# A two-layer hybrid encoder: state space matmuls in line behind the sixth gate, weight splits ranked ahead, outputs grouped by shape, parameters loaded with the projections

## The chip, the cores and the metric

One core of a Trainium2 chip. A core has a matmul engine (TensorE, in rows PE, with PEld for its weight loads), a vector engine (VectorE, DVE), an activation engine (ScalarE, ACT), GpSimd (POOL), and queues that issue DMAs (SyncE, SP, above all). Each engine works through its own list of instructions in order. The metric is the device time of one execution, in microseconds (us).

## The reference, cut to what matters

Two equal layers over a (1, 1024, 1024) float32 input. Each layer takes a root-mean-square norm, one projection to 2504 columns, three token mixers, a SiLU gate on each mixer's output, and one output projection with a residual:

```python
h = rms_norm(x, norm_g[l]); proj = h @ w_in[l]
ya = dsa_branch(...)     # 6 heads, an indexer picks the 256 best keys of each query
yb = s5_branch(u, ...)   # state space: 16 groups of 16 channels, 64 complex states each
yc = mla_branch(...)     # 6 heads, low-rank queries and keys
mixed = concat([ya * silu(ga), yb * silu(gb), yc * silu(gc)])
x = x + mixed @ w_out[l]
```

The state space branch computes, with `abar = exp(a * step)` complex and diagonal, `x_t = abar x_(t-1) + f (B u_t)` and `y_t = Re(C x_t) + D u_t`, then a GELU and a gated linear unit.

## The kernel before, in words

Every matmul of the large projections is split: the float32 weights become a rounded part `whi` and a remainder `wlo`, the activations `hh` and `hl`, and three products are added (`proj_step`, `mm3`). A weight tile arrives by DMA as `raw`; `split_act` (L152) makes `whi` on ACT (L153) and `wlo` on POOL, for some on DVE (L154). `class Stream` (L597) loads the tiles of a layer some four or five ahead and splits them three ahead.

A layer runs so. `norm_tile` and `turn_h` make the transposed `hh` (ACT, L686) and `hl` (DVE, L687) in two halves of four token tiles, `jk` being the normed tile (DVE, L664). `proj_halves` is the first projection, on each half of the tokens in turn. After two projections come the steps of the string `STEPS = "L5C6Q7U01234"` (L49): a letter is a projection, a digit is a gate of 128 channels, and U is the input of the state space branch, two such channels. A gate or U channel has two halves of 24 matmuls of 512 columns (`gt`, L166 to L168). A gate's half is read by ACT (`th`, a tanh, L1182) and by DVE (`gate`, L1183), after which its PSUM bank is free. The tag `s` of PSUM has six banks, shared by projections, gates and later the attention scores; the tag `tr` has two. The sixth gate in this order is "2"; gates "3" and "4" follow it, and then 48 attention items (24 for the indexed heads, then 24 for the latent heads, `scores` and `finish`), and the output projection (`po`).

Beside that run generators, called sides. A side is advanced by `tick` (L574): every projection step, gate matmul group or attention item adds its planned microseconds to a clock, and a side whose due time has come traces its next piece; what it yields is the time until the piece after. One side is the indexer with its search for the 256 best keys (`index_topk`), mostly DVE. Another is the state space branch (`tables_then_s5`, L1189), begun before U; its yields are stretched by `S5M = 1.5`. For each of two halves of the groups, `static` (L401) makes tables (`s5t` on POOL, `s5o`, called `Wf`, on DVE, both at L279), yields `ST3`, and then goes on with matmuls of a 48-column kernel table (L425), the band matrix `M` by DMAs (L437), transposes (L442) and rotation tables on POOL (L264 to L269). `chunks` (L462) makes two PSUM tiles from U (L471), multiplies them by the rotation on DVE (L479 to L486), scans them (L489, L490) and turns them back on POOL to the states `X`; it ends with a yield of `ST2`. `outputs` (L498) adds in PSUM, for each four groups of 16 channels, `U M` (128 rows, L508) and two products of `X` with `Wf` (64 rows, L509, L510), each of which is two passes of the engine, and applies the GELU (ACT L513, L516; DVE L514, L515, L517). When both halves are through, the gated linear unit follows (L547 to L560) and the product with the gate (L1195).

`s5_params` (L285), once in layer 0 for both layers, loads three small tensors by SP (L292) and computes the powers of `abar` in some 125 tiny DVE instructions (tiles `zp`, `s5par`), two memsets on POOL, and stores the result by one DMA (L356). Before the change its loads are traced among the loads of the input, between input tiles 3 and 4, and the rest is a side with due time 1.0. Only the first exponential is held (`issue_after(late[0])`) behind the last `hl` traced until then.

The order on each engine comes from the planner of the framework: it simulates the program on a timeline of its own and lets each engine take, among the instructions whose inputs are there by that timeline, the one of the best rank. The rank is the order of tracing (`tc.cur_priority`, which can be shifted by hand). Where the chip is slower than that timeline, an engine stands before an instruction whose input is late, and all behind it stand too.

Of the kernel before, what the change touches and what calls it, by code (L numbers as in the profile page):

```python
# [24 lines left out]
AHEAD = 3  # L25
DEEP = 2
S5AT = 2
KVAT = 22
KVT = 1.5
EVA = 0.9  # L30
# [19 lines left out]
S5W = (0, 0)  # L50
S5M = 1.5
FT = 0.6
ST2 = 8.0
ST3 = 4.0
GLP = 0
KTP = (0, 0, 0)
# [30 lines left out]
def hybrid_kernel(ctx, tc, A, out, dbg=None, layers=DEPTH):  # L87
# [17 lines left out]
    def ps_s(shape, name="s"):  # L105
        return pp.tile(shape, F32, tag="s", name=name, bufs=BANKS)
# [45 lines left out]
    def split_act(raw, hi, lo, eng=None):  # L152
        S.activation(hi, raw, AF.Copy)  # L153
        (eng or G).tensor_tensor(lo, raw, f(hi), op=ALU.subtract)  # L154
# [130 lines left out]
    def s5_params():  # L285

        zp.clear()
        o = page([128, 1024], F32, "s5par")[:, 0:560].rearrange("p (l c) -> p l c", l=2)

        def load(n):  # L290
            t = tiny("s5" + n)
            nc.sync.dma_start(t, A["ssm_" + n].rearrange("l p g -> p l g"))  # L292
            return t
        ar, ai, ls = (load(n) for n in ("a_re", "a_im", "log_step"))
        yield 0.1
        with tc.issue_after(late[0]):
            step = exp_acc(ls, "ze")
        e1, th = tiny("e1"), tiny("th")
        V.tensor_tensor(e1, ar, step, op=ALU.mult)
        V.tensor_tensor(th, ai, step, op=ALU.mult)  # L300
        yield 2.0
        mag = exp_acc(e1, "zm")
        yield 2.0
        sn, cn = sincos(th, "zs")
        yield 2.0
        abr, abi, den, t1, t2, nr = (tiny(n) for n in ("abr", "abi", "den", "t1", "t2", "nr"))
        fr, fi = o[:, :, 264:272], o[:, :, 272:280]
        V.tensor_tensor(abr, mag, cn, op=ALU.mult)
        V.tensor_tensor(abi, mag, sn, op=ALU.mult)
        V.tensor_tensor(den, ar, ar, op=ALU.mult)  # L310
        V.tensor_tensor(t1, ai, ai, op=ALU.mult)
        V.tensor_tensor(den, den, t1, op=ALU.add)
        V.reciprocal(den, den)
        V.tensor_scalar(nr, abr, -1.0, None, op0=ALU.add)
        V.tensor_tensor(t1, nr, ar, op=ALU.mult)
        V.tensor_tensor(t2, abi, ai, op=ALU.mult)
        V.tensor_tensor(t1, t1, t2, op=ALU.add)
        V.tensor_tensor(fr, t1, den, op=ALU.mult)
        V.tensor_tensor(t1, abi, ar, op=ALU.mult)
        V.tensor_tensor(t2, nr, ai, op=ALU.mult)  # L320
        V.tensor_tensor(t1, t1, t2, op=ALU.subtract)
        V.tensor_tensor(fi, t1, den, op=ALU.mult)
        yield 2.0

        er, ei = (o[:, :, 72 * x:72 * x + 72].rearrange("p l (t g) -> p l t g", g=8) for x in range(2))
        w1, w2 = (tiny(n, 64).rearrange("p (l t g) -> p l t g", l=2, g=8) for n in ("w1", "w2"))
        G.memset(er[:, :, 0, :], 1.0)
        G.memset(ei[:, :, 0, :], 0.0)
        V.tensor_copy(er[:, :, 1, :], abr)
        V.tensor_copy(ei[:, :, 1, :], abi)  # L330
        for n in (1, 2, 4):
            bc = lambda z: z[:, :, n:n + 1, :].to_broadcast([128, 2, n, 8])
            cmul(V, er[:, :, n + 1:2 * n + 1, :], ei[:, :, n + 1:2 * n + 1, :], er[:, :, 1:n + 1, :], ei[:, :, 1:n + 1, :],
                 bc(er), bc(ei), w1[:, :, 0:n, :], w2[:, :, 0:n, :])
        yield 2.0

        q = tiny("q0", 32).rearrange("p (l c) -> p l c", l=2)
        sq = tiny("qq", 32).rearrange("p (l c) -> p l c", l=2)
        V.tensor_copy(q[:, :, 0:8], cn)
        V.tensor_copy(q[:, :, 8:16], sn)  # L340
        for i in range(9):
            if i >= 2:
                n = o[:, :, 144 + 16 * (i - 2):160 + 16 * (i - 2)]
            else:
                n = tiny(f"q{i + 1}", 32).rearrange("p (l c) -> p l c", l=2)
            V.tensor_tensor(sq, q, q, op=ALU.mult)
            V.scalar_tensor_tensor(n[:, :, 8:16], q[:, :, 0:8], 2.0, q[:, :, 8:16], op0=ALU.mult, op1=ALU.mult)
            V.tensor_tensor(n[:, :, 0:8], sq[:, :, 0:8], sq[:, :, 8:16], op=ALU.subtract)
            q = n
            if i % 3 == 2:  # L350
                yield 2.0
        rho = o[:, :, 256:264]
        V.tensor_tensor(rho, mag, mag, op=ALU.mult)
        V.tensor_tensor(rho, rho, rho, op=ALU.mult)
        V.tensor_tensor(rho, rho, rho, op=ALU.mult)
        nc.sync.dma_start(s5_d.rearrange("l p c -> p l c"), o)  # L356
        yield 1.0
# [23 lines left out]
        Z.update(er=er, ei=ei, Br=Br, Bi=Bi, cr=cr, ci=ci, nci=nci, dd=dd, rot=rot, rho=o[:, 256:264])  # L381
        yield 3.0

    def s5(l, Z, us, yb):

        P2 = lambda name: page([128, 2, 4, 8, 16], F32, name)
        j0, j1 = slice(0, 127), slice(1, 128)
# [13 lines left out]
        def static(gh):  # L401
# [5 lines left out]
            eng.tensor_scalar(Wo[:, 1], Wo[:, 1], -1.0, 0.0, op0=ALU.mult, op1=ALU.add)  # L407
            h["Wf"] = Wf = Wo.rearrange("p x g t c -> p x g (t c)")
            yield ST3


            kt = page([128, 8, 128], F32, "s5k")
# [6 lines left out]
            p = ps_tr([128, 4, 128])  # L419
# [78 lines left out]
        def outputs(gh):  # L498

            h = H[gh]  # L500
            U, M, X, Wf = h["U"], h["M"], h["X"], h["Wf"]
            g2 = page([128, 8, 128], F32, "s5g")
            for q in range(2):
                p = ps_s([128, 8, 4, 16])
                for i in range(4):
                    g = 4 * q + i
                    rs, pl = slice(64 * q, 64 * q + 64), i
                    T.matmul(p[:, :, i, :], U[:, g, :], M[:, g, :], start=True, stop=False)  # L508
                    T.matmul(p[:, :, i, :], X[rs, 0, pl, :], Wf[rs, 0, pl], start=False, stop=False)  # L509
                    T.matmul(p[:, :, i, :], X[rs, 1, pl, :], Wf[rs, 1, pl], start=False, stop=True)  # L510
                pf = p.rearrange("p t g c -> p t (g c)")
                y2 = scr([128, 8, 64], F32, "gl")
                S.activation(y2, pf, AF.Square)  # L513
                V.tensor_scalar(y2, y2, 0.044715, 1.0, op0=ALU.mult, op1=ALU.add)  # L514
                V.tensor_tensor(y2, y2, pf, op=ALU.mult)  # L515
                S.activation(y2, y2, AF.Tanh, scale=0.7978845608028654)  # L516
                V.scalar_tensor_tensor(g2[:, :, 64 * q:64 * q + 64], y2, 1.0, pf, op0=ALU.add, op1=ALU.mult)  # L517
                yield 3.0
            yield 1.5
            gt = page([128, 1024], F32, f"s5gT{gh}")  # L520
            for h2 in range(2):
                p = ps_tr([128, 4, 128])
                for i in range(4):
                    T.transpose(p[:, i, :], g2[:, 4 * h2 + i, :], ident)
                S.activation(gt.rearrange("p (j t) -> p t j", t=8)[:, 4 * h2:4 * h2 + 4, :], p, AF.Copy)
                yield 1.0
            yb.append(gt)
# [69 lines left out]
    class Stream:  # L597
# [8 lines left out]
        def split(self, n, how=None):  # L606
            self.load(n)
            while self.raw and len(self.q) < n:
                raw, o = self.raw.pop(0)
                hi, lo = (page(list(raw.shape), F32R, x) for x in ("whi", "wlo"))  # L610
                args = raw[:, :, 0:o], hi[:, :, 0:o], lo[:, :, 0:o]
                if how:
                    how(*args)
                else:
                    split_act(*args, V if len(self.reqs) in WLO else G)
                self.q.append((hi, lo, o))

        def get(self):
# [82 lines left out]
    for t in range(8):  # L701
        xp = page([128, 1024], F32, f"x{t}")
        nc.sync.dma_start(xp, A["x"][0][128 * t:128 * t + 128, :])
        xnew.append(xp)
        if t == 3:
            nc.sync.dma_start(cst_, A["c_all"])
            gains = load_gains(0)
            ws.load(2)
            params = s5_params()
            next(params)  # L710
    htok = [norm_tile(x) for x in xnew[0:4]]
    hT = [[], []]
    turnh = turn_h(0, hT, htok, gains[0])
# [6 lines left out]
    for l in range(layers):  # L720
# [453 lines left out]


        mixf = {}

        def gates(c):
            g = page([128, 1024], F32, f"gate{c}")
# [8 lines left out]

        def tables_then_s5():  # L1189
            yield from s5_tables(l, Z)  # L1190
            for d in s5(l, Z, us, yb):
                yield S5M * d
            for o in range(2):
                gate_in(3 + o)
                (G if GLP else V).tensor_tensor(mixf[3 + o], yb[o], mixf[3 + o], op=ALU.mult)  # L1195
                mixed.add(3 + o)
        if l == 0:
            side(params, 1.0)
        proj_halves(ev_g2)
        proj(ev_iq, tps=range(1, 4), outer="I" not in INNER)  # L1200

# [288 lines left out]
        for i, x in enumerate(STEPS, 8 - len(STEPS)):  # L1490
            at(i)
            if i in QAT:
                next(its)
            if x.isdigit():
                gates(int(x))
            elif x == "U":
                inputs_s5()
            else:
                proj(dict(L=ev_g4, C=ev_g3, Q=ev_g5)[x], outer=x not in INNER)
# [162 lines left out]
```

## Time and profile before

| what | value |
|---|---|
| time, median of 3 runs | 1342.01 us (1340.0 to 1344.65) |
| the profiled execution's own time | 1338.83 us |
| its span | 1337.1 us |
| PE busy | 1245.9 us, 93% |
| PEld busy | 1055.4 us, 79% |
| DVE busy | 877.6 us, 66% |
| ACT, POOL busy | 686.1 us and 676.8 us, 51% each |
| mean granted TensorE clock | 0.973 of full |

Busy is time in which an engine has an instruction under way; its complement is idle time, which the view of waits puts down to whoever ended it. The granted clock is 1.0 at 2.4 GHz and 0.5 at 1.2 GHz.

### The profile page before, as it was taken

To read this page: it belongs to the slowest core of one execution; us is meant where nothing else is said; L and a number is where in the kernel's file an instruction comes from. 1 tells how busy PE (TensorE), PEld (TensorE's weight loads), DVE (VectorE), ACT (ScalarE), POOL (GpSimd) and SP (SyncE) were. 2 spreads that over 40 slices of the span, in tenths; PEclk is the share of its full clock that TensorE was granted. 3 is DMA by queue.
4 is the path that set the end of the run, shared out by engine and by line. 5 is a ranking of instruction groups with operands and counts; after the bars stand their busy time and mean duration, and the time that the engine had idled before them with its cause. 6 is when DMAs were issued, how large, how long until landed. Compare 5 with 4: busy or idle time off the path is not lost. (4 is left out here: it accounts for less than half of the span.)

```text
span 1337.1 us, 23848 instructions
## 1 busy us (share of the span) xinstructions
PE 1245.9 (93%) x8644; PEld 1055.4 (79%) x8644; DVE 877.6 (66%) x2342; ACT 686.1 (51%) x1565; POOL 676.8 (51%) x1112
## 2 busy tenths in 40 slices
PE   5898999699999999999999989997989999999998
PEld 5896898487788778877899879975767786887787
DVE  4968989934786797741253887996366778776121
ACT  5246753021878778752243666412157786877300
POOL 4789159856431457313347963794760335553210
PEclk9898999897999999999999999998979999999999
DMA  6021232322110100241140013133303010004202
GB/s 220 4 71 28 84 110 80 114 75 91 48 54 18 42 27 13 72 175 41 79 145 14 21 60 111 56 105 91 129 13 95 8 55 20 12 31 156 83 32 95
DMA packets 78491, 92.79 MB, mean 69 GB/s; under 512 B 13536, under 2 KB 61280, under 8 KB 78368
## 3 DMA queue, kind: packets, MB, share of 16 engines
q1 hardware_dynamic: 77216, 87.03, 20.3%
q0 software_dynamic: 1152, 4.19, 1.0%
q8 instruction: 68, 1.11, 0.3%
q14 instruction: 55, 0.45, 0.1%
HBM read 63.53 MB, written 26.50 MB: 67 GB/s over the span
## 5 line engine op out<-in xcount | busy, mean ns | idle before, releaser
L758 PE MATMUL pj<-whi,hh 128*128 128x256 f32 (+1 forms) x608 | 173.8, 286 | 0.0
L761 PE MATMUL pj<-whi,hl 128*128 128x256 f32 (+1 forms) x608 | 172.4, 285 | 0.0
L760 PE MATMUL pj<-wlo,hh 128*128 128x256 f32 (+1 forms) x608 | 172.3, 284 | 0.0
L154 POOL TENSOR_TENSOR wlo<-raw,whi 128x1024 fp32r<-128x1024 f32 (+1 forms) x40 | 96.0, 2412 | 144.2 <-ACT whi L153 123.5
L166 PE MATMUL gt<-hh,whi 128*128 128x512 f32 x320 | 130.8, 409 | 0.0
L168 PE MATMUL gt<-hh,wlo 128*128 128x512 f32 x320 | 128.5, 403 | 0.0
L167 PE MATMUL gt<-hl,whi 128*128 128x512 f32 x320 | 128.4, 401 | 0.0
L758 PEld LDWEIGHTS pj<-whi,hh 128*128 128x128 f32 x608 | 118.0, 194 | 1.1 <-issue 0.2
L760 PEld LDWEIGHTS pj<-wlo,hh 128*128 128x128 f32 x608 | 118.0, 194 | 0.7
L761 PEld LDWEIGHTS pj<-whi,hl 128*128 128x128 f32 x608 | 117.4, 194 | 0.3
L1262 ACT ACTIVATE pt<-s 128x512 f32<-128x512 f32 (+1 forms) x154 | 83.1, 555 | 46.3 <-PE s L1256 34.2
L938 DVE SCALAR_TENSOR_TENSOR acc<-rl,iw,acc 128x384 f32<-128x384 f32 (+5 forms) x84 | 93.9, 1120 | 14.3 <-ACT rl L933 11.5
L166 PE MATMUL po<-whi,mix 128*128 128x512 f32 x256 | 98.5, 392 | 1.6 <-DVE gin L1279 1.6
L168 PE MATMUL po<-whi,mix 128*128 128x512 f32 x256 | 99.6, 390 | 0.0
L167 PE MATMUL po<-wlo,mix 128*128 128x512 f32 x256 | 99.6, 390 | 0.0
L1256 PE MATMUL s<-ident,P 128*128 128x128 f32 x588 | 93.5, 275 | 1.6 <-ACT pt L1262 0.9
L1236 ACT ACTIVATE P<-P,nb,qsc 128x1024 f32<-128x1024 f32 (+7 forms) x96 | 82.4, 863 | 16.6 <-DVE nb L1234 16.5
L1579 DVE TENSOR_TENSOR xn<-xn,po 128x512 f32<-128x512 f32 x32 | 22.0, 687 | 103.3 <-PE po L168 92.0
L1182 ACT ACTIVATE th<-gt 128x512 f32<-128x512 f32 x32 | 19.1, 597 | 134.9 <-PE gt L168 49.4
L1236 ACT ACTIVATE P<-P,nb,asum 128x1024 f32<-128x1024 f32 (+7 forms) x96 | 82.4, 864 | 10.6 <-DVE nb L1234 10.3
L933 ACT ACTIVATE rl<-s 128x512 f32<-128x512 f32 (+3 forms) x160 | 74.1, 541 | 24.0 <-PE s L932 15.9
L1226 DVE TENSOR_SCALAR_CACHE_REDUCE P<-s 128x512 f32<-128x512 f32 (+3 forms) x144 | 74.2, 549 | 15.2 <-PE s L1390 11.4
(453 smaller groups left out, 3633.5 us busy)
## 6 DMA issues: line engine op xcount, KB each, us to landing
raw<-in_w_in SPq DMA_DIRECT2D x32, 512.0 KB, 4.5
gate_d<-gate SPq DMA_DIRECT2D x16, 512.0 KB, 2.9
gin<-gate_d SPq DMA_DIRECT2D x16, 512.0 KB, 4.8
raw<-in_w_out SPq DMA_DIRECT2D x16, 512.0 KB, 6.2
x<-in_x SPq DMA_DIRECT2D x8, 512.0 KB, 4.9
cq_d<-cqs SPq DMA_DIRECT2D x16, 256.0 KB, 2.2
cqT<-cq_d POOLq DMA_DIRECT2D x8, 512.0 KB, 6.9
xn<-in_x SPq DMA_DIRECT2D x8, 512.0 KB, 10.1
```

The source lines that it names most:

```text
L154: (eng or G).tensor_tensor(lo, raw, f(hi), op=ALU.subtract)
L166: T.matmul(ps, lh, rh, start=start, stop=False)
L167: T.matmul(ps, lh, rl, start=False, stop=False)
L168: T.matmul(ps, ll, rh, start=False, stop=stop)
L758: T.matmul(o, hk, hi[:, k, 0:n], start=kh == 0 and i == 0 and k == 0, stop=False, skip_group_check=True)
L760: T.matmul(o, hk, lo[:, k, 0:n], start=False, stop=False, skip_group_check=True)
L761: T.matmul(o, lk, hi[:, k, 0:n], start=False, stop=kh == 1 and k == 3, skip_group_check=True)
L938: V.scalar_tensor_tensor(a, r[:, 0:nk], w, a, op0=ALU.mult, op1=ALU.add, **({"accum_out": ssum[:, b - 2:b - 1]} if h == 7 else {}))
L1226: V.tensor_scalar(Ps[j][:, c0:c1], p[:, 0:c1 - c0], 1.0, -3.0e38, op0=ALU.mult, op1=ALU.max, accum_out=m)
L1236: S.activation(Ps[j][:, 0:nk], Ps[j][:, 0:nk], AF.Exp, bias=nb[:, j:j + 1], scale=it["scale"][:, j:j + 1], accum_out=sums[:, j:j + 1])
L1256: T.transpose(p[:, i, :], Ps[j][:, 128 * kt:128 * kt + 128], ident)
L1262: S.activation(pt[:, 0:n, :], p[:, 0:n, :], AF.Copy)
```

## The change

Four edits. (1) `gated` is a list that gets an entry when gate "2" has been traced; `static` polls it each planned microsecond between the tables and the kernel-table matmuls, so that all that follows in the state space side is traced, and thus ranked, behind that gate, in both layers. `ST2` grows from 8 to 10. (2) The split of each streamed weight gets a rank 600 places better. (3) In `outputs`, the four `U M` products of a PSUM tile are issued first and the eight products of `X` behind them; only the first has the start flag. (4) The parameters' loads are traced in the side, and the yield after them is 8.0 in place of 0.1; so the computation comes after at least nine planned microseconds of projection, and `late[0]` is by then the last `hl` of the second half.

```diff
+S5GATE = "2"
+SPLITP = 600
-ST2 = 8.0
+ST2 = 10.0
...
         ar, ai, ls = (load(n) for n in ("a_re", "a_im", "log_step"))
-        yield 0.1
+        yield 8.0
...
             yield ST3
+            while not gated:
+                yield 1.0
...
                 for i in range(4):
-                    g = 4 * q + i
-                    rs, pl = slice(64 * q, 64 * q + 64), i
-                    T.matmul(p[:, :, i, :], U[:, g, :], M[:, g, :], start=True, stop=False)
-                    T.matmul(p[:, :, i, :], X[rs, 0, pl, :], Wf[rs, 0, pl], start=False, stop=False)
-                    T.matmul(p[:, :, i, :], X[rs, 1, pl, :], Wf[rs, 1, pl], start=False, stop=True)
+                    T.matmul(p[:, :, i, :], U[:, 4 * q + i, :], M[:, 4 * q + i, :], start=i == 0, stop=False,
+                             skip_group_check=True)
+                for i in range(4):
+                    for x in range(2):
+                        T.matmul(p[:, :, i, :], X[rs, x, i, :], Wf[rs, x, i], start=False, stop=x == 1,
+                                 skip_group_check=True)
...
+                    tc.cur_priority -= SPLITP
                     split_act(*args, V if len(self.reqs) in WLO else G)
+                    tc.cur_priority += SPLITP
...
-            params = s5_params()
-            next(params)
...
-            side(params, 1.0)
+            side(s5_params(), 1.0)
...
                 gates(int(x))
+                if x == S5GATE:
+                    gated.append(True)
```

## Rows read from the trace of the kernel before

**Rows 1.** Waits of PE: who was waited for, us in total, times, longest.
```profile
PE tr L425 <- DVE s5o L279: 19.8, 2, 9.9
PE tr L683 <- DVE jk L664: 16.1, 4, 7.9
PE s L510 <- POOL s5x L279: 6.3, 2, 3.2
...
PE tr L425 <- POOL s5bd L418: 5.5, 4, 1.8
PE tr L683 <- DVE hl L687: 4.9, 1, 4.9
```

**Rows 2.** Timeline of PE, layer 0: start, us, instruction, idle time before and releaser.
```profile
262.47 0.61 PE L425 MATMUL tr<-s5o,s5bd 128*48 128x112 f32 x2 [9.89 <-DVE s5o L279]
```

**Rows 3.** Busy time by stretch: PE, PEld, DVE, ACT, POOL, PEclk, DMA share, GB/s.
```profile
240.00:260.00 20.00, 10.75 (x48) 8.00 (x48) 19.52 (x29) 3.12 (x5) 19.80 (x21) 0.94 0.40 131
...
280.00:300.00 20.00, 20.00 (x115) 16.19 (x114) 2.73 (x6) 4.80 (x7) 14.16 (x37) 1.00 0.32 92
...
320.00:340.00 20.00, 19.00 (x67) 14.33 (x67) 10.10 (x29) 7.05 (x12) 14.37 (x43) 0.60 0.07 21
...
440.00:460.00 20.00, 20.00 (x158) 15.80 (x158) 12.55 (x56) 15.23 (x44) 9.11 (x23) 1.00 0.22 70
```

**Rows 4.** The same of tile gt alone: PE, PEld, DVE, ACT, PEclk, DMA.
```profile
262.40:313.80 51.40, 46.61 (x188) 36.46 (x188) 5.97 (x9) 4.18 (x7) 0.95 0.31 93
```

**Rows 5.** Tile gt again, at half and at full granted clock.
```profile
263.00:267.60 4.60, 4.59 (x11) 3.63 (x12) 0.00 (x0) 0.00 (x0) 0.50 0.43 119
268.00:273.00 5.00, 5.00 (x23) 3.97 (x22) 0.00 (x0) 0.60 (x1) 1.00 0.01 3
```

**Rows 6.** Timeline of DVE at the end of the key search, layer 0.
```profile
274.64 0.69 DVE L1183 SCALAR_TENSOR_TENSOR gate<-th,gt 128x512 f32<-128x512 f32 x1 [1.84 <-POOL wlo L154]
...
275.85 0.68 DVE L1183 SCALAR_TENSOR_TENSOR gate<-th,gt 128x512 f32<-128x512 f32 x1
...
286.63 1.89 DVE L1183 SCALAR_TENSOR_TENSOR gate<-th,gt 128x512 f32<-128x512 f32 x3 [4.24 <-DVEq L1058]
```

**Rows 7.** Timeline of PE in outputs of the first half, half clock.
```profile
321.18 0.80 PE L508 MATMUL s<-s5m,s5U 128*128 128x128 f32 x2
...
323.06 0.79 PE L508 MATMUL s<-s5m,s5U 128*128 128x128 f32 x2
```

**Rows 8.** Timeline of PE in outputs of the second half, full clock.
```profile
423.11 0.49 PE L508 MATMUL s<-s5m,s5U 128*128 128x128 f32 x2
423.52 0.49 PE L509 MATMUL s<-s5o,s5x 64*128 64x128 f32 x2
...
424.16 0.66 PE L1249 MATMUL acc_o<-pt,va 128*64 128x128 f32 x8
```

**Rows 9.** Timeline of DVE at the first attention items of layer 0.
```profile
327.60 0.46 DVE L514 TENSOR_SCALAR gl<-gl 128x512 f32<-128x512 f32 x1 [12.42 <-ACT gl L513]
```

**Rows 10.** Timeline of DVE at the start.
```profile
14.67 1.42 DVE L310 TENSOR_TENSOR zp<-zp 128x16 f32<-128x16 f32 x1 [5.35 <-DMA zp<-in_ssm_a_re]
...
16.84 0.74 DVE L664 TENSOR_SCALAR jk<-x,rst 128x1024 f32<-128x1024 f32 x1
```

**Rows 11.** Timeline of POOL at the start.
```profile
14.19 1.87 POOL L150 TENSOR_TENSOR wlo<-raw,whi 128x800 fp32r<-128x800 f32 x1
```

**Rows 12.** Timeline of PE: the first projection matmul.
```profile
21.27 0.50 PE L758 MATMUL pj<-whi,hh 128*128 128x200 f32 x1
```

**Rows 13.** Busy time of tile zp alone: PE, PEld, DVE, ACT, POOL.
```profile
28.00:66.00 38.00, 0.00 (x0) 0.00 (x0) 18.93 (x124) 0.00 (x0) 0.00 (x0) 0.91 0.00 1
```

**Rows 14.** Timeline of SP's queue at the start.
```profile
11.93 0.51 SPq L292 DMA_DIRECT2D zp<-in_ssm_a_re  x1
```

**Rows 15.** Line 279, table products on DVE: ns min/median/max, first and last start.
```profile
L279 DVE TENSOR_TENSOR s5tab<-zp x16: 667/758/2822, 254.4 to 995.2; 128x512 f32<-128x512 f32 x16
```

**Rows 16.** Timeline of DVE: last product of the state space branch, layer 1.
```profile
1132.65 1.21 DVE L1195 TENSOR_TENSOR gin<-s5gT,gin 128x1024 f32<-128x1024 f32 x1
```

**Rows 17.** Timeline of PE: first matmul of the output projection, layer 1.
```profile
1239.55 0.48 PE L166 MATMUL po<-whi,mix 128*128 128x512 f32 x1
```

More of the change, by code (lines that the diff above doesn't have):

```diff
@@ L382, in s5_tables, with s5 @@
         yield 3.0
-    def s5(l, Z, us, yb):
+    def s5(l, Z, us, yb, gated):
         P2 = lambda name: page([128, 2, 4, 8, 16], F32, name)
@@ L504, in outputs @@
                 p = ps_s([128, 8, 4, 16])
+                rs = slice(64 * q, 64 * q + 64)
                 for i in range(4):
-                    g = 4 * q + i
-                    rs, pl = slice(64 * q, 64 * q + 64), i
-                    T.matmul(p[:, :, i, :], U[:, g, :], M[:, g, :], start=True, stop=False)
-                    T.matmul(p[:, :, i, :], X[rs, 0, pl, :], Wf[rs, 0, pl], start=False, stop=False)
-                    T.matmul(p[:, :, i, :], X[rs, 1, pl, :], Wf[rs, 1, pl], start=False, stop=True)
+                    T.matmul(p[:, :, i, :], U[:, 4 * q + i, :], M[:, 4 * q + i, :], start=i == 0, stop=False,
[4 more added lines that the diff above has]
+                                 skip_group_check=True)
                 pf = p.rearrange("p t g c -> p t (g c)")
@@ L1176, in hybrid_kernel @@
         mixf = {}
+        gated = []
         def gates(c):
@@ L1190, in tables_then_s5 @@
             yield from s5_tables(l, Z)
-            for d in s5(l, Z, us, yb):
+            for d in s5(l, Z, us, yb, gated):
                 yield S5M * d
```

## The prediction

> **What bounds the kernel now.** I read the page's shares first, then the waits of PE, then the busy time in stretches of 20 us, then the timelines around PE's longest waits. PE is the engine to watch: through the attention it has no idle time at all (20.00 of 20 us, where DVE has 12.55) [rows 3]. So what can be won is PE's idle time, time at half clock, and time that PE itself wastes. The waits stand in few places [rows 1]: 19.8 us in two waits of L425 for `s5o`, one in each layer [rows 2], 5.5 us of L425 for `s5bd`, 6.3 us of L510 for `s5x`, and at the start 16.1 and 4.9 us of the transposes L683. The first stands in a stretch where PE is busy for 10.75 of 20 us and DVE for 19.52 [rows 3]: DVE is deep in the key search, its part of the state space tables comes late, and gate matmuls that need neither stand behind L425. After such a wait the granted clock is half (1.2 GHz): 0.50 from 263.0 to 267.6, where 11 `gt` matmuls take 4.60 us, against 23 in 5.00 us at full clock [rows 5].
>
> **Edit 1, the state space matmuls behind gate "2".** *Gain at most.* The two kinds of L425 wait sum to 25.3 us [rows 1]. The half clock costs 11 x (0.418 - 0.217) = 2.2 us [rows 5], taken for each layer: 4.4. Together 29.7.
>
> *What is late next.* A gate's bank is freed by DVE, and the six banks of tag `s` hold just the six halves of gates "0", "1" and "2". In layer 0 the first of them is freed from 274.64, the second from 275.85, the next three only from 286.63, behind the key search's branch [rows 6]. When the long wait ended, 188 `gt` matmuls were left [rows 4], 96 of them of gates "3" and "4"; so 92 x 0.217 = 20.0 us to the end of gate "2". Begun 9.89 us before 262.47 [rows 2] they end at 272.6, and with the 2.75 us a layer of `s5bd` waits gone at 269.8. Gate "3" then waits for a bank until 274.64: 4.8 us, or 3.0 if the 1.84 us for `wlo` [rows 6] go, since that chain hung on the stalled PE. The kernel-table matmuls, now ranked here, fill some of it. Gate "3" takes 48 x 0.217 = 10.4 us, to about 285, and gate "4" waits some 2.3 us for the third bank (286.63 + 0.69). Given back: about 5 us a layer, so 29.7 - 10 = **20 us**. Bounds: 29.7 if DVE frees banks in time; about 6 if both waits for banks come in full, halve the clock again, and the search ends late.
>
> *At the attention's start.* The outputs of the first half now stand, with L510's wait for `s5x`, between the last gate and the attention: DVE waits 12.42 us in `gl` there [rows 9], and the granted clock of that stretch is 0.60 [rows 3]. Behind the gate, and with `ST2` 2 x 1.5 = 3 planned us longer, they fall among attention items, where PE finds other work. The waits are 6.3 us [rows 1]. At half clock a triple (L508, L509, L510) takes 323.06 - 321.18 = 1.88 us [rows 7], at full 424.16 - 423.11 = 1.05 [rows 8]; with five triples a layer at half clock (an estimate, of eight) that is 10 x 0.83 = 8.3. Together 14.6 at most, zero at least. The attention's first items no longer overlap with that work, so part of it turns into the start-up of their own pipeline; I take **10**.
>
> *Does the later end matter?* The side moves by some 30 planned us. In layer 1 its last product is at 1132.65 and the output projection begins at 1239.55 [rows 16, 17], so over 100 us are left.
>
> **Edit 3, grouping.** From L508 to L509 two passes take 0.41 us, from L509 to L1249 four passes 0.64 [rows 8]; as passes plus one change of shape that is 0.115 us a pass and 0.18 a change. A PSUM tile has seven changes inside it now and one after: 6 x 0.18 = 1.1 us, and eight tiles in two layers, 8.6. It is PE's own time in a stretch where PE is the bound, so it counts in full where the planner doesn't set other work between: **7**, bounds 0 and 8.6.
>
> **Edit 4, parameters.** DVE stands 5.35 us before L310, a parameter product whose DMA is late, and then runs such products; the third norm product starts only at 16.84 [rows 10]. PE's transposes wait for it (the longest of 7.9 and others [rows 1]), and the first projection matmul is at 21.27 [rows 12]. Without it the next that is late is the first weight remainder, done at 14.19 + 1.87 = 16.06 [rows 11]: 5.2 us gained. The three loads leave SP's queue ahead of input tiles 4 to 7, which are then issued some 3 x 0.5 us sooner [rows 14]. The parameter chain, 18.93 us of DVE in 38 [rows 13], is now ranked behind the second half's `hl`, which PE waited 4.9 us for [rows 1]; it falls on the following projection, with the two POOL memsets, and its store goes later in SP's queue, where the next weight loads may then pass it instead of standing behind it. Most of the 5.2 + 4.9 then meets the indexer and the key search, which are DVE's; I take **6**, bounds 0 (another late DMA, as three loads still feed DVE in order) and 13 (both, and 3 us of half clock).
>
> **Edit 2, splits ahead, and what the move costs: -4.** PE never waited for a split in these rows, so this gains only as cover for a faster PE. Two things speak against. Ranked ahead, ACT may stand before a `whi` whose DMA is late. And POOL's remainder runs next to DVE's work: a table product of 128x512 on DVE took 667 ns at least and 2822 at most [rows 15]. The Trainium skill, page "SBUF — State Buffer", section "Who interferes with whom", says that a DVE instruction with two SBUF inputs and a GpSimd one that reads SBUF exclude each other for a whole instruction; the trace agrees with that in its spread, and were every one of the sixteen table products to meet a split, the rule would make the sum below about 8 us instead of 39. From the row alone, a product that meets one pays at most 2822 - 667 = 2155 ns; with half of the sixteen that is -17, and with none 0. I take -4, nearer to none, since the median of the row is 758 ns.
>
> **Sum.** 20 + 10 + 7 + 6 - 4 = 39 us off the profiled execution (its span of 1337.1 and 1.7 around it, which stay): 1338.83 - 39 = 1299.8. The median of the runs lies 3.2 us above that execution (1342.01), so 1303.
>
> **Rivals.** (a) *DVE and the banks set the gates' end* (chance 0.18). For it: DVE at 19.52 of 20 before, and the release at 286.63. Then edit 1 gives 6 and 5, the rest as above: 6 + 5 + 7 + 6 - 4 = 20, 1322. Against it: DVE is busy for only 2.73 of 20 us from 280 on.
> (b) *The planner undoes it* (0.08). Its timeline, not the chip's, orders PE; if it sets L425 into the wait for a bank, PE stands there before the same late `s5o`, and parameter products may still slip ahead of the norm. Edit 1 then gives 5 + 5, edit 3 still 7, edit 4 nothing: 17 - 4 = 13, 1329.
> (c) *Slower: DVE becomes the bound of the attention* (0.07). State space work that ran under gates, where DVE was nearly idle, moves among items whose scores DVE has to read in order. If PE waits on DVE there, about 11 us of DVE work a layer (the two stretches from 280 and 320 hold 12.83 us, with some attention in it) come on top, and L510's waits appear once more: 22 + 6.3 - 7 - 6 = 15 slower, 1357. It decides once DVE's share in the attention passes PE's; 12.55 against 20.00 speaks against it.
>
> **How the numbers follow.** The forecast has 0.64, (a) 0.18, (b) 0.08, (c) 0.07, and 0.03 remain for no difference by several small losses. All upper bounds together are 29.7 + 14.6 + 8.6 + 13 = 66, which is 1276; I don't expect them all, so the range begins at 1281, and it ends at 1332, past (b). About 4 us (0.3%) can't be told from no change. Faster: the forecast, (a), (b) but for a part: 0.89; same 0.04; slower 0.07.
>
> **What would show it.** Right: no wait of L425 near 10 us; gates "3" and "4" ending some 10 us sooner against the search's end; no 12 us wait of DVE for `gl`; one change of shape in a PSUM tile; no wait of DVE for `in_ssm_a_re` before the norm; PE's idle time down by 25 us or more and the granted clock above 0.98. Wrong: long waits of `gt` for DVE's L1183 (a), of L425 or DVE for the same things elsewhere (b), or waits of `acc_o` and scores for DVE in the attention (c).

## The result: slower by 1.2%

| | median us | range | ratio to before, 95% interval |
|---|---|---|---|
| before | 1341.0 | 1338.8 to 1344.7 | |
| changed | 1354.5 | 1351.7 to 1360.3 | 1.012, 1.0093 to 1.0146 |

The forecast was 1303 and faster. The changed kernel is slower, at the time of rival (c). The profiled execution took 1354.69 us, its span 1352.9. PE's busy time is the same (1245.2 us after, 1245.9 before), so what grew is its idle time, from 91 to 108 us. The equal busy time hides two things that go against each other: the grouping of edit 3 by itself takes 13.2 us off it (run c3 below, 1232.7), and the gate of edit 1 by itself adds 9.0 (run a3, 1254.9).

The waits of PE in the changed kernel (who waited for whom, us in total, times, longest) answer to [rows 1]:

```profile
PE gt L170 <- POOL wlo L156: 22.1, 2, 11.1
PE tr L1263 <- ACT P L1243: 13.1, 2, 6.5
PE s L1395 <- DVE P L1233: 8.8, 2, 4.4
PE tr L691 <- DVE jk L672: 8.5, 3, 7.5
...
PE kv L168 <- DVE s5g L523: 4.4, 2, 2.9
...
PE tr L691 <- DVE hl L695: 1.6, 1, 1.6
```

The waits for `s5o`, `s5bd` and `s5x` are gone, as the change says, and the start's waits are shorter (`jk` 8.5 for 16.1, `hl` 1.6 for 4.9). In their place stand a wait of the gate matmuls for a weight remainder, longer than the one removed, and waits in the attention that were not there.

Where the time lies is seen best by stages of layer 0: the gates (from the 97th `gt` matmul, the first of gate "7", through U to the last of gate "4"), the indexed heads (to the last `acc_o<-pt,va`) and the latent heads (to the last `acc_o<-pt,vc`). Columns: stretch, its length, then busy us and instructions of PE, PEld, DVE, ACT and POOL, granted clock, DMA share, GB/s. Before:

```profile
203.50:313.80 110.30, 97.64 (x466) 78.72 (x464) 82.67 (x161) 23.91 (x42) 79.95 (x120) 0.95 0.32 97
313.80:467.20 153.40, 146.89 (x1174) 115.78 (x1172) 106.82 (x361) 107.27 (x256) 60.04 (x119) 0.94 0.14 44
467.20:604.80 137.60, 132.91 (x1126) 112.00 (x1124) 92.57 (x334) 97.57 (x241) 59.29 (x112) 1.00 0.19 70
```

After:

```profile
195.60:300.30 104.70, 93.63 (x433) 76.56 (x433) 78.21 (x153) 23.41 (x41) 77.81 (x117) 0.95 0.35 106
300.30:447.50 147.20, 132.91 (x1147) 106.44 (x1148) 108.36 (x365) 103.53 (x252) 63.53 (x122) 0.97 0.12 36
447.50:611.20 163.70, 152.35 (x1185) 123.35 (x1183) 100.80 (x339) 101.09 (x246) 59.60 (x111) 0.97 0.19 65
```

The start gains 7.9 us, the gates 5.6, the indexed heads 6.2; then the latent heads take 26.1 us more, and all of it is lost. Layer 1 does the same (gates 109.8 to 104.5, indexed 156.9 to 149.9, latent 138.0 to 161.1). What changed places is the end of the state space branch. The glu matmuls of layer 0 (duration ns min/median/max, first and last start), before and after:

```profile
L547 PE MATMUL glu<-s5gT,wglu x16: 590/592/697, 446.2 to 465.6; 128*128 128x512 f32 x16
```

```profile
L553 PE MATMUL glu<-s5gT,wglu x16: 590/592/595, 488.2 to 507.8; 128*128 128x512 f32 x16
```

Before they end with the indexed heads; after, they and the second half's outputs stand wholly among the latent heads. Yet the indexed heads' stretch got only 6.2 us shorter.

Three waits of after in detail. First the gates. Timelines (start, us, instruction) of ACT, of POOL and of PE:

```profile
234.52 1.05 ACT L155 ACTIVATE whi<-raw 128x1024 fp32r<-128x1024 f32 x1
```

```profile
246.31 2.48 POOL L281 TENSOR_TENSOR s5tab<-zp 128x512 f32<-128x512 f32 x2
248.76 2.87 POOL L156 TENSOR_TENSOR wlo<-raw,whi 128x1024 fp32r<-128x1024 f32 x1
```

```profile
251.68 0.80 PE L170 MATMUL gt<-hh,wlo 128*128 128x512 f32 x1 [11.07 <-POOL wlo L156]
```

PE reaches the remainder of the next weights at 240.6, and POOL, without a gap since before that, works through ropes, search copies and tables first. `whi`, which the remainder is made from, was there at 235.57, 13 us before POOL took it up: the better rank of edit 2 did not bring this split forward. In the stretch of [rows 3] at 240 PE is busy for 8.93 of 20 us now, at a granted clock of 0.74, half speed behind the wait. Second, DVE and PE at the attention's start:

```profile
302.26 0.69 DVE L483 TENSOR_TENSOR s5tab<-vr,s5R 128x512 f32<-128x512 f32 x1 [0.57 <-PE vi L475]
...
306.02 0.69 DVE L487 TENSOR_TENSOR s5tab<-vi,s5R 128x512 f32<-128x512 f32 x1
...
307.83 1.22 DVE L493 TENSOR_TENSOR_SCAN s5z<-s5rho,s5z 128x512 f32<-128x512 f32 x1
...
315.25 1.22 DVE L494 TENSOR_TENSOR_SCAN s5z<-s5rho,s5z 128x512 f32<-128x512 f32 x1
...
317.09 0.80 DVE L1239 TENSOR_TENSOR mx<-mx 128x2 f32<-128x2 f32 x1
317.81 0.15 DVE L1241 SCALAR_TENSOR_TENSOR nb<-mx,asum 128x2 f32<-128x2 f32 x1
```

```profile
319.38 0.47 PE L1263 MATMUL tr<-ident,P 128*128 128x128 f32 x1 [6.55 <-ACT P L1243]
```

The first chunk's eight DVE instructions (six of 0.69, two of 1.22: 6.6 us) run between the first scores' readings, ahead of the `nb` that the first exponential needs. Before, they began at 300.98, under the gates, which ended at 313.8. Third, among the latent heads:

```profile
528.39 1.25 DVE L1202 TENSOR_TENSOR gin<-s5gT,gin 128x1024 f32<-128x1024 f32 x1
531.46 2.56 DVE L1344 TENSOR_TENSOR kt<-kt,kr__7063 128x256 f32<-128x256 f32 x1 [1.82 <-POOL kr__7063 L165]
...
534.15 0.41 DVE L1344 TENSOR_TENSOR kt<-kt,kr__7063 128x256 f32<-128x256 f32 x1
...
534.69 1.21 DVE L1202 TENSOR_TENSOR gin<-s5gT,gin 128x1024 f32<-128x1024 f32 x1
535.82 0.68 DVE L1233 TENSOR_SCALAR_CACHE_REDUCE P<-s 128x512 f32<-128x512 f32 x1
```

```profile
531.39 2.35 POOL L156 TENSOR_TENSOR mix<-gin,mix 128x1024 fp32r<-128x1024 f32 x1
```

The late products of the branch (L1202) and the split of their result on POOL stand ahead of a score that PE waits 4.39 us for.

### The profile page after: what moved, and what is told of

It is laid out like the page before. It is cut to its first block, busy times and chain, and to the rows that moved or that the text cites. A ratio compares the mean times of both kernels' runs of the same rounds, so it can differ in the third digit from the quotient of the medians.

```text
span 1352.9 us, 23859 instructions
## 1 busy us (share of the span) xinstructions
PE 1245.2 (92%) x8644; PEld 1052.0 (78%) x8644; DVE 885.5 (65%) x2342; ACT 685.3 (51%) x1565; POOL 681.8 (50%) x1112
## 5 line engine op out<-in xcount | busy, mean ns | idle before, releaser
L170 PE MATMUL gt<-hh,wlo 128*128 128x512 f32 x320 | 127.7, 401 | 22.1 <-POOL wlo L156 22.1
L1263 PE MATMUL s<-ident,P 128*128 128x128 f32 x588 | 99.5, 285 | 3.1 <-ACT pt L1269 1.6
L1243 ACT ACTIVATE P<-P,nb,qsc 128x1024 f32<-128x1024 f32 (+7 forms) x96 | 82.3, 865 | 19.8 <-DVE nb L1241 19.7
L170 PEld LDWEIGHTS gt<-hh,wlo 128*128 128x128 f32 x320 | 62.0, 194 | 36.1 <-POOL wlo L156 23.0
L939 ACT ACTIVATE rl<-s 128x512 f32<-128x512 f32 (+3 forms) x160 | 74.0, 536 | 23.7 <-PE s L938 15.4
L1285 DVE TENSOR_TENSOR gin<-acc_o,gin 128x128 f32<-128x128 f32 x96 | 27.6, 288 | 88.3 <-PE acc_o L1282 87.5
```

Of the source, the lines that this page charges most:

```text
L170: T.matmul(ps, ll, rh, start=False, stop=stop)
L939: S.activation(r[:, c0:c1], p[:, 0:c1 - c0], AF.Relu)
L1243: S.activation(Ps[j][:, 0:nk], Ps[j][:, 0:nk], AF.Exp, bias=nb[:, j:j + 1], scale=it["scale"][:, j:j + 1], accum_out=sums[:, j:j + 1])
L1263: T.transpose(p[:, i, :], Ps[j][:, 128 * kt:128 * kt + 128], ident)
```

## The experiments

All times are medians, ratios against runs of the kernel before on the same chip. "Theory" and "rival" in the expectations are those of the time; the table at the end of this section gives the stages.

**Undoing and isolating.** *a1: edit 1 undone.*

```diff
-ST2 = 10.0
+ST2 = 8.0
-        gated = []
+        gated = [True]
```

> The changed kernel with edit 1 undone: the state space matmuls wait for no gate and ST2 is 8.0 again; split rank, grouping and parameters stay. Theory (the late state space work is what costs: its DVE products and its outputs fall into the attention, 16 to 20 us a layer there): the attention goes back to about 291 us a layer from gates' end to latent heads' end, the two waits of 9.9 us for s5o come back, and the time is some 1341 - 8 (parameters) - 5 (grouping) = 1328, range 1320 to 1336. Rival (the split rank is what costs): the time stays at or above 1345. Rival (grouping holds the PSUM banks longer): 1341 or more.

Measured 1321.6, ratio 0.9874 (0.9857 to 0.989). The gate costs, and edits 2 to 4 gain 16.6 us together. The 9.9 us waits for `s5o` are back (19.8 in two), and the kernel is still 33 us quicker than with the gate.

*a2: the split rank undone.*

```diff
-SPLITP = 600
+SPLITP = 0
```

> The changed kernel with SPLITP = 0: the weight splits stand in their own rank again. Theory (late state space work): nothing won, 1350 to 1362, and the 11.1 us waits of gt for wlo stay or grow. Rival (the split rank costs, by ACT and POOL standing before attention work): 1341 or less.

Measured 1350.8, 1.0104 (1.0085 to 1.0124): the rank isn't the cause. Without it the wait for the remainder is 8.3 us, not 11.1, so in the gates the rank costs a little; the whole times differ by 2 us by the ratios, which is within the noise.

*a3: edit 1 alone, on the kernel before* (`S5GATE = "2"`, `ST2 = 10.0`, the wait in `static`, as in the diff).

> The kernel before with edit 1 alone (gate 2 and ST2 = 10). Theory (late state space work): slower than the whole change, since the gains of parameters and grouping lack: 1354.5 + 8 + 5 = 1367, range 1358 to 1374. Rivals (split rank or grouping cost): 1341 or less, as the long wait for s5o is gone.

Measured 1363.7, 1.0195 (1.0178 to 1.0212): 25.5 us slower, as the theory said.

*a4: the gate kept, the longer pace undone* (`ST2 = 8.0`).

> The changed kernel with ST2 = 8.0, the gate kept. Theory (the place of the chunk products behind the last gate costs, not the three planned us of ST2): 1349 to 1358, the 6.5 us wait of the first P transposes unchanged. Rival (ST2 pushes the outputs late): 1340 or less.

Measured 1348.2, 1.0095 (1.0067 to 1.0123), a little under the theory's range, with the 6.5 us wait unchanged. The gate, not the pace, makes most of it.

**Where the gate stands.** *b1 and b2: the gate at "0" and at "1", both with* `ST2 = 8.0`.

```diff
-S5GATE = "2"
+S5GATE = "0"    # b2: "1"
```

> The changed kernel with S5GATE = 0 and ST2 = 8.0: the state space matmuls stand behind the fourth gate instead of the sixth, two gates earlier. Theory (what costs is that the first half's chunk products come only behind the last gate, so that their DVE work meets the attention's start and all later state space work slides by 20 us): they run under the last gates again, the 6.5 us wait of the first P transposes is gone, 1316 to 1330. Rival (any gate costs, because the planner then orders the attention more finely): 1340 or more.

> The changed kernel with S5GATE = 1 and ST2 = 8.0: behind the fifth gate. Theory: in between, with chunk products near gates' end but still ahead of the first scores, 1318 to 1340. Rival (any gate costs): 1340 or more, as with gate 2 (1348).

Measured 1329.0 (0.9932, 0.9905 to 0.9958) and 1344.0 (1.0041, 1.0019 to 1.0063). b2 is a miss for the theory as I had put it: its chunk matmuls run at 294.7, ahead of the first scores at 302.2, the 6.5 us wait is gone, and it is as slow as with gate "2". So the collision at the start isn't the main part. What grows with the gate is the latent heads' stretch: 139.3 us without, 145.3, 154.2, 158.5 behind "0", "1", "2".

**The DVE work by itself.** *b3 and b4: six of eight DVE instructions a chunk left out, with the gate and without.*

```diff
-            V.tensor_tensor(xa, vr, RR, op=ALU.mult)
-            V.tensor_tensor(xb, vi, RI, op=ALU.mult)
+            V.tensor_tensor(zr, vr, RR, op=ALU.mult)
...
-            V.tensor_tensor_scan(fl(zr), fl(RH), fl(zr), 0.0, op0=ALU.mult, op1=ALU.add)
-            V.tensor_tensor_scan(fl(zi), fl(RH), fl(zi), 0.0, op0=ALU.mult, op1=ALU.add)
```

> The changed kernel (gate 2, ST2 = 10) with six of the eight DVE instructions of each chunk left out (four products and both scans, some 4 x 0.69 + 2 x 1.22 = 5.2 us a chunk; two products stay, so the state space part isn't computed). Theory (this DVE work at the attention's start is a main part of the cost): the 6.5 us wait of the first P transposes falls under 2, and with two chunks a layer the time falls by 10 to 18 us, to 1336 to 1344. Rival (only the place of the PE work counts): 1350 to 1356.

> The same six DVE instructions a chunk left out where the gate is undone (run before: 1321.6). Theory: the first chunk's work lies under the gates there and is free, the second's hides behind PE: 1316 to 1323. Rival (that DVE work costs wherever it stands): 1306 to 1312.

Measured 1342.7 (1.0031, 1.0017 to 1.0046) and 1312.5 (0.9806, 0.9776 to 0.9836): 11.8 us gained with the gate, 9.1 without. b3 is in its theory's range, but the wait of the first P transposes fell to 3.1 us, not under 2. b4 is just above its rival's range: this work costs nearly as much where the tuned place has it, and of the gate's 33 us only some 3, a difference that isn't clear of the noise, can be put down to its new place. A second thing is seen in the indexed heads' stretch, b3 and then b4:

```profile
303.00:441.00 138.00, 129.06 (x1144) 104.95 (x1144) 98.82 (x349) 103.36 (x253) 63.15 (x125) 0.98 0.14 38
```

```profile
310.70:452.40 141.70, 137.01 (x1174) 109.86 (x1173) 102.67 (x355) 107.01 (x257) 55.57 (x114) 0.99 0.15 45
```

Against the change it shrinks by 9.2 us (147.2 to 138.0) with 9.5 us of DVE less (108.36 to 98.82), against a1 by 5.5 (147.2 to 141.7) with 4.8 less (107.46 in a1), while PE's matmuls stay the same. There leaving out DVE's work gains about one for one, though DVE is busy for only some 70% of the stretch. Part of the gain is on PE: its busy time falls by 3.9 us (from 132.91) and by 2.7 (from 139.66 in a1), at a granted clock of 0.98 for 0.97 and of 0.99 for 0.97. Whether the clock rose because PE waited less, no run separates.

**The other edits, and earlier or quicker branches.** *c1: grouping and parameters alone* (a1 with `SPLITP = 0`).

> Grouping and parameters alone (no gate, ST2 = 8.0, SPLITP = 0). With the split rank the same kernel took 0.9874 of before. Theory (the split rank gives nothing; without it the changed kernel was 3.8 us quicker): 1314 to 1322. Rival (the split rank earned part of the 16.6 us): 1324 to 1332.

Measured 1315.1, 0.9829 (0.9808 to 0.9849): the quickest kernel here that leaves out no work (b4 took 1312.5 without six DVE instructions a chunk), 23 us under before and 39 under the change. The split rank costs 6 us there.

*c2: no gate, outputs earlier* (a1 with `ST2 = 4.0`).

> The changed kernel without the gate and with ST2 = 4.0: outputs stand 4 x 1.5 = 6 planned us earlier than in the kernel with 8.0, twice a layer. Theory (the later the state space tail falls into the attention, the more it costs; 453 to 470 to 485 to 506 us for glu's end gave 1322, 1329, 1344, 1348): at or under 1321. Rival (there is a best place, and earlier outputs stand with their wait for s5x ahead of the attention): 1326 to 1336.

Measured 1352.6, 1.0101 (1.0082 to 1.0121). "The later, the dearer" falls, and the time is beyond the rival's range too: 6 planned us earlier cost 31 us against a1. Stretches of layer 0 (gates' end to the last `va`, then to the last `vc`):

```profile
313.50:470.20 156.70, 145.05 (x1178) 114.84 (x1176) 110.66 (x368) 108.88 (x259) 64.55 (x127) 0.95 0.17 51
470.20:611.90 141.70, 134.56 (x1111) 114.01 (x1111) 88.59 (x327) 95.24 (x238) 55.45 (x102) 0.96 0.19 68
```

The latent heads are near their 139 us, and the indexed heads take 9 to 12 us more than in a1 and c1.

*c3: the grouped outputs alone, on the kernel before.*

> The kernel before with the grouped outputs alone. PE's own time in the two kinds of output matmuls was 41.8 us before and 25.0 with grouping and no gate, so up to 16.8 us if PE's order stays: theory 1325 to 1333. Rival (that time lies where PE would wait anyhow, at half clock ahead of the attention): 1334 to 1339.

Measured 1323.5, 0.9891 (0.9871 to 0.991): 14.5 us, a little more than expected.

*c4: gate "2", with a quicker pace behind it.*

```diff
-ST2 = 10.0
-ST0 = 3.0
-ST1 = 5.0
+ST2 = 2.0
+ST0 = 1.0
+ST1 = 1.0
```

> The changed kernel, gate 2 kept, with the pace behind the gate raised: ST2 = 2.0, ST0 = ST1 = 1.0, by which the second half's outputs and the glu stand some 48 planned us earlier. Theory (the state space tail that slid from among the indexed heads to among the latent heads, where PE has no time to give, is the larger part of the cost): glu ends before 475 in layer 0, and the time is 1325 to 1338 though the first chunk's products still meet the attention's start. Rival (the gate and the collision at the attention's start are the cost): 1345 or more.

Measured 1347.4, 1.0063 (1.0043 to 1.0084), a miss: glu ends at 442, the latent heads are back at 143.6 us, but the indexed heads take 160.2, with waits that the changed kernel doesn't have, for the GELU, for states and for tables:

```profile
PE s L1419 <- DVE s5g L523: 8.0, 4, 2.4
PE s L515 <- POOL s5x L281: 7.6, 4, 3.4
...
PE s L511 <- POOL s5tab L281: 4.4, 2, 2.2
```

**A shift without a gate, and one place alone.** All three stand on c1. *d1:* `ST2 = 10.0`. *d2:* `S5AT = 3`. *d3: the tail alone later:*

```diff
         yield from chunks(1)
+        yield 24.0
         yield from outputs(1)
```

> Grouping and parameters alone (1315.1, 0.983 of before) with ST2 = 10.0 instead of 8.0: outputs 3 planned us later, no gate. Theory A (every piece of state space work has a place against the attention's items, and a shift of a few planned us costs): 1320 to 1340. Theory B (only a shift of the gate's size costs): 1312 to 1319.

> Grouping and parameters alone with S5AT = 3: all state space work starts one step of the gates' list later, with no gate that its matmuls wait for. Theory A (lateness against the attention costs, whatever causes it): 1325 to 1350, with A's and C's idle time up as under the gate. Theory B (the gate itself, which lets tables run ahead and holds only matmuls, costs): 1310 to 1320.

> Grouping and parameters alone with 24 x 1.5 = 36 planned us put ahead of the second half's outputs: the start stays, the last outputs and the glu move from among the indexed heads to among the latent heads. Theory A (the tail's place is the larger part of the cost): glu ends near 490 in layer 0, the latent heads' part grows by some 15 to 24 us a layer and the indexed heads' part shrinks by less than 10: 1325 to 1345. Theory B (the same work only changes its place): 1312 to 1319.

Measured 1333.8 (0.9965, 0.9948 to 0.9982), 1356.7 (1.0133, 1.0108 to 1.0158) and 1347.5 (1.008, 1.005 to 1.0111), against 1315.1. Theory A in all three, though d2 and d3 cost more than its ranges: no gate is needed to lose the time. Three planned us cost 18 us; a branch begun one step later costs 41, about as much as the gate; and the tail's later place alone costs some 34. The two attention stretches of layer 0 in c1, then in d3:

```profile
307.00:451.80 144.80, 137.57 (x1174) 110.36 (x1172) 107.02 (x361) 106.88 (x256) 61.39 (x119) 0.99 0.15 46
451.80:591.10 139.30, 134.60 (x1124) 113.45 (x1124) 92.57 (x334) 97.36 (x241) 59.23 (x112) 0.99 0.20 69
```

```profile
305.60:444.80 139.20, 128.50 (x1112) 103.68 (x1111) 102.75 (x352) 102.25 (x252) 61.93 (x121) 0.96 0.14 40
444.80:606.20 161.40, 153.83 (x1188) 122.98 (x1187) 103.90 (x342) 101.58 (x245) 59.65 (x110) 0.97 0.20 66
```

Some 62 instructions of PE go from one to the other. The stretch that they leave gets 5.6 us shorter, nearer to the 4.3 us of DVE work that left with them than to their own 12; the one that they join gets 22.1 longer. There PE's busy time rises by 19.2 us: some 13 are the moved matmuls (glu 6.9, outputs 5.9, by the time each adds to PE's), the rest is time at half clock (0.97 for 0.99) and slower matmuls of the heads themselves. No run moves the tail without letting the planner order the heads' instructions anew around it, so how much of the 22.1 beyond the moved matmuls is the place, and how much the new order, stays open.

*d4: the changed kernel with the branch ranked behind the attention* (`S5P = 200`).

> The changed kernel with S5P = 200: all state space instructions ranked 200 behind, so that DVE takes scores ahead of chunk products. Theory (the collision at the attention's start costs, about 6.5 us a layer of PE's wait): the wait of the first P transposes falls under 2 us, 1338 to 1348. Rival (what DVE doesn't do there it has to do a little later, and PE waits for that): 1350 to 1360.

Measured 1351.8, 1.0098 (1.0072 to 1.0124): its rival. The first wait shrinks, and others take its place:

```profile
PE s L1419 <- DVE mx L1235: 5.6, 6, 1.1
...
PE tr L1263 <- ACT P L1243: 2.9, 2, 1.4
```

**A try for more.** *e2: c1 with the gate at "0"; e1: the same with* `ST0 = 2.0, ST1 = 3.0`.

> A try at a version that beats both: grouping and parameters, no split rank, the matmuls behind gate 0 (with it gates took 109 us a layer, and the tail straddled the border between indexed and latent heads: glu 448 to 470), and ST0 = 2.0, ST1 = 3.0, which bring the first chunks 6 and the tail 12 planned us forward. Theory (the tail's place decides): glu ends near 455 in layer 0, the latent heads' part is back at 139 to 141 us, 1308 to 1320. Rival (the finer places decide, and a quicker pace meets s5x and s5tab that aren't ready, as with ST2 = 2 and 4): 1325 to 1350.

> Grouping and parameters, no split rank, matmuls behind gate 0, the old pace. With the split rank it took 1329.0; the rank's part is 4 to 6 us: 1321 to 1326 in theory, above the 1315.1 without a gate, as the tail still straddles the border. Rival (no gate effect left without the rank): 1313 to 1317.

Measured 1328.4 (0.9904, 0.9875 to 0.9932) and 1326.4 (0.9894, 0.9864 to 0.9924). With glu ending at 448, latent heads at 142.2 and indexed at 152.2, e1 is the same sum in another split (e2: 145.4 and 147.5). e1 is in its rival's range, e2 at the top end of its theory's; neither beats c1.

Stages of layer 0 in us, and the end of glu:

| run | median | gates | indexed | latent | glu ends |
|---|---|---|---|---|---|
| before | 1341.0 | 110.2 | 153.5 | 137.6 | 466 |
| changed | 1354.5 | 104.6 | 147.3 | 163.7 | 508 |
| a1 no gate | 1321.6 | 112.8 | 147.2 | 139.3 | 453 |
| a2 no rank | 1350.8 | 101.7 | 150.6 | 163.4 | 507 |
| a3 gate alone | 1363.7 | 102.6 | 148.7 | 163.9 | 516 |
| a4 ST2 8 | 1348.2 | 105.1 | 148.1 | 158.5 | 506 |
| b1 gate "0" | 1329.0 | 108.9 | 147.3 | 145.3 | 470 |
| b2 gate "1" | 1344.0 | 106.9 | 147.5 | 154.2 | 486 |
| c1 grouping, parameters | 1315.1 | 110.6 | 144.8 | 139.3 | 451 |
| c2 earlier | 1352.6 | 115.8 | 156.7 | 141.8 | 449 |
| c3 grouping | 1323.5 | 110.2 | 148.1 | 139.0 | 461 |
| c4 quick | 1347.4 | 107.8 | 160.2 | 143.6 | 442 |
| d1 | 1333.8 | 110.1 | 152.4 | 141.7 | 473 |
| d2 | 1356.7 | 106.9 | 148.4 | 158.8 | 490 |
| d3 | 1347.5 | 109.9 | 139.2 | 161.4 | 508 |

## Why the prediction was wrong

**The step that failed** is "Does the later end matter?". It measured the branch's end against its due time, found "over 100 us are left" [rows 16, 17], and priced the move at nothing. The slack is real: after, the last product is at 1198.08 and the output projection begins at 1255.38. But slack against the end is not room on PE. With the gate alone (a3) the indexed and the latent heads of layer 0 take:

```profile
305.10:453.80 148.70, 134.47 (x1148) 106.48 (x1148) 108.22 (x365) 103.42 (x252) 63.34 (x122) 0.97 0.12 35
453.80:617.70 163.90, 153.65 (x1185) 123.44 (x1183) 100.99 (x339) 100.83 (x246) 59.81 (x111) 0.98 0.19 65
```

Against before, 12.4 us of PE's busy time left the first stretch, which gave back 4.7; the second got 20.7 us more of it and took 26.3 longer (layer 1: 14.1 and 7.0, 21.6 and 27.1). d3 shows the tail's move by itself: some 34 us, where 37 separate a2 from c1 (1.0104 against 0.9829). That doesn't make the tail the cause of all but 3: d3 leaves the gates as they were. By stages of both layers, the gate (a2 against c1) costs 55 us in the attention and gives 16 in the gates and 4 at the fronts; d3 costs 31 in the attention. So some 25 us of the 55 are left for what else the gate moves, above all the first half's later start, which no run has by itself (d2 moves the tail too). How they split isn't settled: the new place of the chunks' DVE work makes some 3 (b3, b4), and taking the wait at the start away gave 2.7 (d4), neither clear of the noise.

**"At the attention's start", 10 us of gain.** L510's waits went, as it said, and DVE's 12.42 us for `gl` [rows 9] too. But the sentence that part of it "turns into the start-up" was mis-sized: the first P transposes wait 6.55 us. Over both layers, the gate alone (a3) changed the attention from 586.0 to 627.6 us: -10 was +41.6. Of the signs the prediction named, the waits of L425, of `gl` and for `in_ssm_a_re` went, but PE's idle time is up by 16.5 us where it was to fall by 25, and the granted clock is 0.970, not above 0.98.

**Edit 1 in the gates, 20 us.** Measured alone 220.0 to 204.6 us over both layers: 15.4. The mechanism given for what is late next was not the one: no gate matmul waits for a bank, and in layer 0 DVE frees them from 265.7 on. What is late is POOL's remainder. "PE never waited for a split in these rows" was true only because PE stood still for `s5o` until 262.47 while POOL caught up (its remainder was done at 258.1); it was the 1.84 us row for `wlo` in [rows 6] that showed POOL behind.

**Edit 3, 7 us.** The mechanism was right: in the changed kernel a tile's sixteen second matmuls follow each other.

```profile
474.72 0.61 PE L511 MATMUL s<-s5m,s5U 128*128 128x128 f32 x4
475.26 2.05 PE L515 MATMUL s<-s5o,s5x 64*128 64x128 f32 x16
477.24 0.50 PE L1395 MATMUL s<-kc0h,qT 104*128 104x512 f32 x1
```

Alone it gained 14.5 us (c3): the term took full clock for all eight tiles, and four of them ran at half [rows 7], where the same matmuls take nearly double. The first half's outputs of layer 0 stood from 313.6 to 332.4, and grouped (c3) from 313.8 to 324.4; but then PE waits 3.0 us for the GELU of the same outputs, so the next score comes at 327.38 for 332.42, 5 us sooner:

```profile
327.38 0.77 PE L1414 MATMUL s<-ka_hi,qA 128*128 128x512 f32 x1 [3.00 <-DVE s5g L519]
```

In the gated kernel there is less to gain, since the gate already takes most of these matmuls off half clock: their busy time is 47.0 us before, 38.2 with the gate alone (a3), 27.0 in the change. Grouping, parameters and rank together gain some 9 to 10 us there (a3 to the change), 16.6 without the gate.

**Edit 4, 6 us.** About 8 (c1 less c3). The first projection matmul is at 14.08 for 21.27 [rows 12]:

```profile
14.08 0.36 PE L764 MATMUL pj<-whi,hh 128*128 128x200 f32 x1 [0.77 <-POOL whi L151]
```

**Edit 2, -4.** -6 without the gate (a1 less c1), right in sign and size; with it -2 by the ratios, within the noise. The reason given wasn't seen: table products (L281) on DVE are no slower (median 682 ns for 758 [rows 15], at most 2826 for 2822). What does cost the 6 us stays open.

**Rival (c)** had the end, 1357, and the place, the attention; its argument against was the weak link. It said that one window's shares, 12.55 for DVE and 20.00 for PE [rows 3], speak against DVE as a bound. They don't: in b3 and b4 the indexed heads get shorter with less DVE work all the same, and as chunk products came in there while the tail went out (DVE 106.8 us before, 108.4 after), that stretch gave little back. But the rival had only half of it: the other half is PE's, among the latent heads, and its condition, DVE's share passing PE's, never came about. Shares couldn't have told the two stretches apart: before, PE is busy for 96% of the indexed heads' stretch and 97% of the latent heads'.

## What to carry to other kernels

Price a move by what it leaves and what it joins: the time that a stretch gives back when work leaves it and the time that another takes when it arrives are two numbers, and a far deadline says nothing of either. A branch woven into an in-order stream by a planner's pace has a tuned place, from which both earlier (c2) and later (d1, d2, d3) cost here; change one edit at a time there, and try the move first with a delay alone, as d3 does. Of this change, keep the grouping and the parameters, and leave the gate and the rank: 1315.1 us, 0.983 of before.

## What the runs showed of the hardware

A DVE product of 128x256 took 2.56 us at 531.46 and 0.41 at 534.15 (shown above); the slow one ran while POOL's `mix` did, from 531.39 for 2.35 us. At 317.09 a product of two columns took 0.80 us (shown above too) and ended at 317.89, as POOL's rotation product did, begun at 316.61 for 1.26; the same line at 331.94, where POOL runs nothing, took 0.16:

```profile
331.94 0.16 DVE L1239 TENSOR_TENSOR mx<-mx 128x2 f32<-128x2 f32 x1
```

```profile
316.61 1.26 POOL L281 TENSOR_TENSOR s5tab<-s5z,s5R 128x508 f32<-128x508 f32 x1 [3.75 <-DVE s5z L494]
```

The Trainium skill, page "SBUF — State Buffer", section "Who interferes with whom", says that a DVE instruction with two SBUF inputs contends with a GpSimd one that reads SBUF; both pairs of rows agree, and add that even a two-column product pays the other's remaining time.
